# Retention in spans of 256 tokens, with the decay folded into the values and divided out by the head norm

## The chip, the cores and the metric

The kernel runs on one core of one Trainium2 chip, as one launch. The metric is device microseconds of that core, from the first to the last instruction of one execution; each kernel is run several times, and the median counts. One execution of each kernel is also recorded by the hardware profiler; all durations of single instructions are from that execution.

Five engines work side by side and wait for each other through semaphores: TensorE (PE, the matrix engine, with its weight load PEld), VectorE (DVE), ScalarE (ACT), GpSimd (POOL) and SyncE (SP, which here issues the DMA transfers). Matrix products are accumulated in PSUM banks of 128 x 512 float32.

## The reference

One encoder block on x [1, 1024 tokens, 1024], float32: a half-weighted SwiGLU, a token-mixing layer, a second half-weighted SwiGLU, a final norm. The change touches retention, in the token-mixing layer. It has 4 heads of 256 columns. Per head, with g = 1 - 2^(-5-h):

```
q = rotary(q); k = rotary(k) * 256**-0.5            # [1024, 256] each
inner_decay = g ** |n - m|     inside a chunk of 64 tokens
inner  = (q_chunk @ k_chunk.T * inner_decay) @ v_chunk
cross  = (q_i * g**(i+1)) @ state                   # state: 256 x 256
state  = state * g**64 + (k_i * g**(63-i)).T @ v_chunk
ret    = inner + cross
ret    = ret * rsqrt(mean(ret**2 over the head's 256) + 1e-6)
ret    = ret * silu(g_ret)
```

Written without the recurrence: token n of the output sums over every token m of its own chunk and of all chunks before, weighted by g^|n-m|. How many tokens are taken by the direct form (scores) and how many through the state is free, so long as whole chunks are kept together. After that `ret @ w_ret_up` and a pooling branch are merged by gates and go through an output projection.

## The kernel before, in words

Each matmul is done as three products of split operands (`mm3`, lines 159 to 163: high by high, high by low, low by high), so "one product" below is three matmul instructions. An operand is split by a CAST on ACT (line 141) and a subtraction on DVE (line 142), or, scaled on the way, by lines 145 (ACT) and 146 (DVE).

The stages in order are: SwiGLU 1, the projections (the last of them v), retention with the pooling branch beside it, the merge, the output projection (its first product is `ru0a`), SwiGLU 2. This text is about the retention stage. q, k, v and the swish gate g lie in DRAM and are loaded by head.

Retention goes by units: a head h and a half nh of the tokens (512), eight units in all, named by both digits ("20" is head 2, first half). For a unit the kernel before does:

- scores (line 1045): four key blocks of 128 tokens against the queries from that block on, 512, 384, 256 and 128 wide, two contractions of 128 each. Each goes to one bank `s`; DVE multiplies it by the decay (line 1053, `sc`), and it is split (`sm`).
- keys, first half only: `by_token` (line 996) transposes k into banks `kd..b` and splits it times a power of the decay; values: v likewise into banks `v..b` (transposes on PE against the identity `cst`).
- inner: ten blocks of scores by values, 256 wide, into two banks `ob`.
- across: in the first half the state `st` (keys by values, 8 products), in the second half the cross sum `xb` (queries by state, 8 products) in two banks of its own.
- outputs: in the first half ACT copies `ob` (line 1095); in the second ACT scales `xb` by the decay's power (line 1098) and DVE adds `ob` (line 1100). Then ACT sums squares (line 1103).
- after the second half, normalise: a reciprocal root by a few operations on [128 x 8] tiles, and eight scalings of the output on DVE (line 1110).
- finish, one unit later: the gate is loaded into a tile `rg`, the outputs are transposed in 16 transposes into four banks `ot` (line 1121), DVE multiplies bank by gate (line 1122), the result is stored to DRAM (`ret`) and loaded again by `take` for the output projection.

What sets the order: `Flow.run` (lines 51 to 81) takes steps of two parts, a preparation and a body, and runs each body four steps after its preparation, with some background work between. A scheduler then sets the order on each engine by its own picture of time, so two steps can be interleaved. Between the steps of retention stand fillers that need nothing of it: the pooling branch, 20 steps of 24 matmuls 512 wide each (4 of `px`, and 16 that make up `pu0` to `pu7`); their results are multiplied by a gate `pg` on DVE (line 975). In the kernel before one filler stands between the scores and the values of a unit, and one more behind `rest` in the first three units.

Memory that is handed round: six PSUM banks ("ps") for everything named above, two more ("sum") for running sums; in SBUF three tiles of tag `tl` (a unit's q, k and v, and the two gate tiles `rg` of a head), nine of tag `t4` (split scores, the state, the outputs, the reloaded `ret`), four of tag `raw` (weights before their split, gates `pg`), ten of tag `c2`. A tile's new owner waits until the old one's readers are done. All loads and stores named here are issued from SP, in order (line 129); a load whose tile is not free holds what is behind it.

Of the kernel before, what the change touches and what calls it, by code (L numbers as in the profile page):

```python
# [42 lines left out]
C_ID, C_ONE, C_CNT, C_KDEC, C_QDEC = 0, P, 2 * P, 2 * P + 64, 2 * P + 80  # L43
NC = 2 * P + 96
# [40 lines left out]
def block_kernel(ctx: ExitStack, tc, x, x_tok, vecs, f1_in, f1_out, w_in, pool_w, w_ret, w_pool, w_o,  # L85
# [98 lines left out]
    def inverse_root(sums, n, name):  # L184
# [7 lines left out]
        nc.vector.tensor_scalar(v, sums, 1.0 / n, EPS, MUL, ADD)  # L192
# [7 lines left out]
        tt(r, r1, t, MUL)  # L200
        return r
# [785 lines left out]
    def by_token(get, scale, name):  # L987

        slots = []
        for jj in range(2):  # L990
            b = bank(f"{name}b{jj}")
            m = mv(f"{name}{jj}")
            for z in range(2):
                for i in range(2):
                    j = 2 * jj + z
                    nc.tensor.transpose(b[:, z * HD + i * P : z * HD + (i + 1) * P], get(i)[:, j * P : (j + 1) * P],
                                        ident)
            for z in range(2):
                sl = slice(z * HD, (z + 1) * HD)
                split_scaled(m[:, 0, sl], m[:, 1, sl], b[:, sl], scale(2 * jj + z))  # L1000
            slots.append(m)
        return slots

    def col(t, n):
        return t[:, n : n + 1]

    class Unit:


        def __init__(self, h, nh):  # L1010
            self.h, self.nh, self.name = h, nh, f"{h}{nh}"

        def loads(self):
# [3 lines left out]
            for n, spilled in (("v", vs), ("q", qs), ("k", ks)):  # L1017
                r = self.src[n] = tl(f"{n}{self.name}")
                for i in range(2):
                    load(half(r, i), spilled[2 * self.h + i][:, at])  # L1020
            if self.nh == 0:
                self.dec = sb.tile([P, H], F32, tag="dec", bufs=1, name=f"dec{self.h}")
                load(self.dec, decay[self.h])
                self.ss = sb.tile([P, 8], F32, tag="ss", bufs=2, name=f"ss{self.h}")
                self.O = {}

        def follow(self, u):

            self.dec, self.ss, self.O, self.state = u.dec, u.ss, u.O, u.state

        def values(self):
            self.V = by_token(lambda i: half(self.src["v"], i), lambda j: col(mix.r_tok, 4 * self.nh + j),
                              f"v{self.name}")

        def keys(self):

            self.kd = by_token(lambda i: half(self.src["k"], i), lambda j: col(cst, C_KDEC + 4 * self.h + j),
                               f"kd{self.h}")
# [5 lines left out]
        def scores(self):  # L1044
            self.sm = []
            for j in range(4):
                wid = H - j * P
                b = bank(f"s{self.name}{j}")
                for i in range(2):
                    mm3(b[:, :wid], parts(self.K[i], slice(j * P, (j + 1) * P)), parts(self.Q[i], slice(j * P, H)),  # L1050
                        i == 0, i == 1)
                c = c2(f"sc{self.name}{j}")
                tt(c[:, :wid], b[:, :wid], self.dec[:, :wid], MUL)
                m = sb.tile([P, 2, H], F32R, tag="t4", bufs=N_T4, name=f"sm{self.name}{j}")
                split(m[:, 0, :wid], m[:, 1, :wid], c[:, :wid])
                self.sm.append(m)

        def cell(self, banks, t):
            return banks[t // 2][:, (t % 2) * HD : (t % 2 + 1) * HD]

        def v(self, j, at=None):
            o = (j % 2) * HD
            return parts(self.V[j // 2], slice(o, o + HD))

        def inner(self):
            self.ob = [bank(f"ob{self.name}{z}") for z in range(2)]
            for j in range(4):
                for t in range(j, 4):

                    mm3(self.cell(self.ob, t), parts(self.sm[j], slice((t - j) * P, (t - j + 1) * P)), self.v(j),  # L1070
                        j == 0 and t % 2 == 0, j == t)

        def across(self):
            if self.nh == 0:
                b = bank(f"st{self.h}")
                for i in range(2):
                    for j in range(4):
                        o = (j % 2) * HD + i * P
                        mm3(b[:, i * HD : (i + 1) * HD], parts(self.kd[j // 2], slice(o, o + P)), self.v(j),
                            i == 0 and j == 0, j == 3)  # L1080
                self.state = sb.tile([P, 2, H], F32R, tag="t4", bufs=N_T4, name=f"state{self.h}")
                split(self.state[:, 0], self.state[:, 1], b)
            else:
                self.xb = [bank(f"xb{self.h}{z}") for z in range(2)]
                for t in range(4):
                    for i in range(2):
                        mm3(self.cell(self.xb, t), parts(self.Q[i], slice(t * P, (t + 1) * P)),
# [279 lines left out]
```

## Time and profile before

| what | value |
| --- | --- |
| median of three runs | 2215.68 us (2214.87 to 2216.01) |
| span of the profiled execution | 2216.0 us |
| PE busy | 2192.6 us (99%), 10092 matmuls |
| DVE busy | 1637.3 us (74%) |
| ACT busy | 968.1 us (44%) |
| granted TensorE clock, mean of the span | 0.996 |
| retention stage: first transposes of v to the first `ru0a` | 1179.13 to 1402.80 us |

The profiled execution has no time of its own beside its span; the span of 2216.0 us stands 0.3 us above the median of the three runs.

How to read it: PE has hardly a gap over the whole span, so the time is the sum of what PE does, of the few times it waits, and of stretches at a lower clock. Matmuls are pipelined: one starts before the last has ended, so what a matmul costs is the distance from its start to the next one's start, and not its own duration. The view of windows gives busy time by engine for a stretch, with the granted clock (PEclk, 1.00 is full) and the DMA share; the view of waits says which engine waited for what, in total, how many times, and the longest; the timeline gives start, duration, engine, line, operation, and in brackets the idle time before and who ended it.

### The profile page before, as it was taken

The numbers are of one execution on the slowest core, as the hardware profiler recorded it, in microseconds if no ns is written. First come the engines' busy times: TensorE is split into PE (matmuls) and PEld (weight loads), VectorE is DVE, ScalarE is ACT, GpSimd is POOL, SyncE is SP. The second block draws the span as 40 slices with busy tenths as digits, with TensorE's granted clock in tenths as the row PEclk, the third lists the DMA queues.
The fourth block names the chain that finished last, engine by engine and source line by source line (L and its number), as shares of the span: only waits on it lengthen the run. The fifth ranks groups of instructions, "written<-read, shape, count | busy, mean of one in ns | idle before, by whom it ended". The sixth has DMA issues, their size and how long they took to land.

```text
span 2216.0 us, 27375 instructions
## 1 busy us (share of the span) xinstructions
PE 2192.6 (99%) x10092; PEld 1827.2 (82%) x10092; DVE 1637.3 (74%) x2706; ACT 968.1 (44%) x1722; POOL 0.2 (0%) x4
## 2 busy tenths in 40 slices
PE   9999999999999999999999999999999999999998
PEld 7888888888888888888888788888888888888887
DVE  8787777887696676777868567685876767788775
ACT  7533333455563434333437454443533333344451
POOL 0000000000000000000000000000000000000000
PEclk9999999999999999999999999999999999999999
DMA  5243232585323333232336457364132322249522
GB/s 209 95 162 138 91 124 91 181 309 190 114 96 128 124 114 124 96 129 80 133 114 215 127 181 262 105 218 134 57 143 100 123 92 103 95 159 330 181 89 77
DMA packets 109863, 311.87 MB, mean 141 GB/s; under 512 B 12320, under 2 KB 14496, under 8 KB 109728
## 3 DMA queue, kind: packets, MB, share of 16 engines
q1 hardware_dynamic: 109728, 310.12, 40.4%
q8 instruction: 79, 1.29, 0.2%
q14 instruction: 56, 0.46, 0.1%
HBM read 219.37 MB, written 90.70 MB: 140 GB/s over the span
## 4 chain that ended last, share of the span: by engine, by line
PE 97%; DVE 1%; DMA 1%; ACT 1%; issue 0%; SPq 0%; DVEq 0%; ACTq 0%
PE c_b L161 3%; PE c_b L162 3%; PE c_b L163 3%; PE a_b L161 3%; PE a_b L162 3%; PE a_b L163 3%; PE c_a L161 2%; PE a_a L162 2%; PE c_e L163 2%; PE c_a L163 2%; PE c_e L162 2%; PE a_e L162 2%; PE a_a L161 2%; PE a_e L161 2%; PE c_a L162 2%; PE a_a L163 2%
## 5 line engine op out<-in xcount | busy, mean ns | idle before, releaser
L141 ACT CAST c_wS<-c_S 128x512 fp32r<-128x512 f32 x88 | 54.7, 622 | 132.3 <-PE c_b L163 76.2
L141 ACT CAST a_wS<-a_S 128x512 fp32r<-128x512 f32 x84 | 52.3, 622 | 106.7 <-PE a_b L163 71.6
L142 DVE TENSOR_TENSOR c_wS<-c_S,c_wS 128x512 fp32r<-128x512 f32 x88 | 60.8, 691 | 25.1 <-ACT c_wS L141 24.5
L142 DVE TENSOR_TENSOR a_wS<-a_S,a_wS 128x512 fp32r<-128x512 f32 x84 | 58.0, 691 | 24.1 <-ACT a_wS L141 23.7
L161 PE MATMUL c_a<-n3R,c_wL 128*128 128x512 f32 x176 | 68.6, 390 | 0.0
L161 PE MATMUL c_b<-n3T,c_wS 128*128 128x512 f32 x176 | 68.5, 389 | 0.0
L163 PE MATMUL c_b<-n3T,c_wS 128*128 128x512 f32 x176 | 68.5, 389 | 0.0
L162 PE MATMUL c_b<-n3T,c_wS 128*128 128x512 f32 x176 | 68.5, 389 | 0.0
L162 PE MATMUL c_a<-n3R,c_wL 128*128 128x512 f32 x176 | 68.5, 389 | 0.0
L163 PE MATMUL c_a<-n3R,c_wL 128*128 128x512 f32 x176 | 68.5, 389 | 0.0
L161 PE MATMUL a_a<-n1R,a_wL 128*128 128x512 f32 x168 | 65.8, 391 | 0.0
L163 PE MATMUL a_a<-n1R,a_wL 128*128 128x512 f32 x168 | 65.4, 389 | 0.0
L162 PE MATMUL a_a<-n1R,a_wL 128*128 128x512 f32 x168 | 65.4, 389 | 0.0
L161 PE MATMUL a_b<-n1T,a_wS 128*128 128x512 f32 x168 | 65.4, 389 | 0.0
L162 PE MATMUL a_b<-n1T,a_wS 128*128 128x512 f32 x168 | 65.4, 389 | 0.0
L163 PE MATMUL a_b<-n1T,a_wS 128*128 128x512 f32 x168 | 65.4, 389 | 0.0
L141 ACT CAST c_wL<-c_ra 128x512 fp32r<-128x512 f32 x44 | 27.3, 621 | 44.2 <-PE c_e L163 38.0
L141 ACT CAST a_wL<-a_ra 128x512 fp32r<-128x512 f32 x42 | 26.0, 622 | 38.3 <-PE a_e L163 38.3
L142 DVE TENSOR_TENSOR c_wL<-c_ra,c_wL 128x512 fp32r<-128x512 f32 x44 | 30.4, 691 | 11.7 <-ACT c_wL L141 11.4
L162 PEld LDWEIGHTS c_b<-n3T,c_wS 128*128 128x128 f32 x176 | 33.0, 188 | 6.9
L161 PEld LDWEIGHTS c_b<-n3T,c_wS 128*128 128x128 f32 x176 | 33.0, 188 | 6.9
L162 PEld LDWEIGHTS c_a<-n3R,c_wL 128*128 128x128 f32 x176 | 33.0, 188 | 6.8
(2377 smaller groups left out, 7255.4 us busy)
## 6 DMA issues: line engine op xcount, KB each, us to landing
c_ra<-in_f_in SPq DMA_DIRECT2D x22, 512.0 KB, 3.6
c_rb<-in_f_in SPq DMA_DIRECT2D x22, 512.0 KB, 4.8
a_ra<-in_f_in SPq DMA_DIRECT2D x21, 512.0 KB, 3.7
a_rb<-in_f_in SPq DMA_DIRECT2D x21, 512.0 KB, 5.1
t<-au SPq DMA_DIRECT2D x11, 512.0 KB, 2.7
b<-an SPq DMA_DIRECT2D x11, 512.0 KB, 3.2
r<-au SPq DMA_DIRECT2D x11, 512.0 KB, 3.8
br<-r SPq DMA_DIRECT2D x11, 512.0 KB, 5.7
```

Source lines behind the costliest of these rows:

```text
L141: copy(hi, src)
L142: tt(lo, src, hi.bitcast(F32), SUB)
L161: mm(dst, w[0], m[0], start=start, stop=False, skip_group_check=True)
L162: mm(dst, w[0], m[1], start=False, stop=False, skip_group_check=True)
L163: mm(dst, w[1], m[0], start=False, stop=stop, skip_group_check=True)
```

## The change

The retention of a unit is cut into two spans of 256 tokens.

- Scores are only taken inside a span: two key blocks in each, so per unit one bank `sa` (256 wide twice) and one bank `sb` (128 wide twice), instead of four banks.
- All that comes before the span goes through the state. For every span but a head's first, queries by state are added into the same bank `ob` that holds the inner sum, so `xb`, its scaling (line 1098) and the addition (line 1100) are gone. For every span but a head's last, keys by values are added to the state's sum, which stays in one "sum" bank over a whole head; after each span it is split into operands (`state`).
- This needs no decay in between: v is scaled by g^-m (n counted from the middle of the head's 1024 tokens), plain k and q are used, the output comes out times g^-n, and the head norm divides it by its own root mean square. `inverse_root` gets two more [128 x 8] operations so that the epsilon is still right. The decay table of the scores now holds only what differs inside a span (the two-sided decay of a chunk, and zeros).
- Keys are transposed for three of four spans of a head (12 transposes, not 8).
- The order by steps is new: first span of unit n, scores of n+1, second span of n, transposes (values and keys) of n+1, then fillers (two behind each of the first two units, one behind the others), then `finish` of the head before. Four fillers stand ahead of the first unit.
- The gate tiles `rg` are taken from `t4`, not `tl`, but for the last head; the last head's result stays in SBUF and is not stored and loaded again.

The diff, cut to its core:

```diff
-        nc.vector.tensor_scalar(v, sums, 1.0 / n, EPS, MUL, ADD)
+        if by is None:
+            nc.vector.tensor_scalar(v, sums, 1.0 / n, EPS, MUL, ADD)
+        else:
+            tt(v, sums, by[0], MUL)
+            nc.vector.tensor_scalar(v, v, EPS, None, ADD)
...
+        if by is not None:
+            tt(r, r, by[1], MUL)
...
-            for n, spilled in (("v", vs), ("q", qs), ("k", ks)):
+            for n, spilled in (("q", qs), ("k", ks), ("v", vs)):
...
         def scores(self):
-            self.sm = []
-            for j in range(4):
-                wid = H - j * P
-                b = bank(f"s{self.name}{j}")
+            a, b = bank(f"sa{self.name}"), bank(f"sb{self.name}")
+            for dst, j, wid in ((a, 0, 2 * P), (b, 1, P)):
+                for z in range(2):
+                    o = (2 * z + j) * P
+                    for i in range(2):
+                        mm3(dst[:, z * wid : (z + 1) * wid], parts(self.K[i], slice(o, o + P)),
+                            parts(self.Q[i], slice(o, o + wid)), z == 0 and i == 0, i == 1)
...
+            tt(ca, a, self.dec, MUL)
...
+            split(self.sa[:, 0], self.sa[:, 1], ca)
+            split(self.sb[:, 0], self.sb[:, 1], cb[:, :HD])
...
+        def turned(self):
+            if self.nh == 0:
+                tt(self.vs, mix.r_tok, head(C_VDEC, self.h), MUL)
+            self.V, self.kt = [], []
+            for n, slots in (("v", self.V), ("k", self.kt)):
+                src = self.src[n]
+                for z in range(2):
+                    if n == "k" and self.nh == 1 and z == 1:
+                        continue
+                    b = bank(f"{n}t{self.name}{z}")
+                    m = mv(f"{n}t{self.name}{z}")
+                    for t in range(2):
+                        for i in range(2):
+                            o = (2 * z + t) * P
+                            nc.tensor.transpose(b[:, t * HD + i * P : t * HD + (i + 1) * P], half(src, i)[:, o : o + P],
+                                                ident)
+                    if n == "k":
+                        split(m[:, 0], m[:, 1], b)
+                    else:
+                        for t in range(2):
+                            sl = slice(t * HD, (t + 1) * HD)
+                            split_scaled(m[:, 0, sl], m[:, 1, sl], b[:, sl], col(self.vs, 4 * self.nh + 2 * z + t))
+                    slots.append(m)
...
+        def span(self, z, state, states):
+            ob = bank(f"ob{self.name}{z}")
+            for j, t, m, o in ((0, 0, self.sa, 2 * z * P), (0, 1, self.sa, 2 * z * P + P), (1, 1, self.sb, z * P)):
+                mm3(self.cell(ob, t), parts(m, slice(o, o + P)), parts(self.V[z], slice(j * HD, (j + 1) * HD)),
+                    j == 0 and t == 0, j == t and state is None)
+            if state is not None:
+                for t in range(2):
+                    o = (2 * z + t) * P
+                    for i in range(2):
+                        mm3(self.cell(ob, t), parts(self.Q[i], slice(o, o + P)),
+                            parts(state, slice(i * HD, (i + 1) * HD)), False, i == 1)
+            last = self.nh == 1 and z == 1
+            if not last:
+                begun = state is not None
                 for i in range(2):
-                    mm3(b[:, :wid], parts(self.K[i], slice(j * P, (j + 1) * P)), parts(self.Q[i], slice(j * P, H)),
-                        i == 0, i == 1)
...
-        def inner(self):
-            self.ob = [bank(f"ob{self.name}{z}") for z in range(2)]
-            for j in range(4):
-                for t in range(j, 4):
...
+                    for j in range(2):
+                        o = j * HD + i * P
+                        mm3(self.cell(states, i), parts(self.kt[z], slice(o, o + P)),
+                            parts(self.V[z], slice(j * HD, (j + 1) * HD)), not begun and i == 0 and j == 0, j == 1)
+                state = sb.tile([P, 2, H], F32R, tag="t4", bufs=N_T4, name=f"state{self.name}{z}")
+                split(state[:, 0], state[:, 1], states)
+            if z == 0:
+                self.O[self.nh] = t4(f"o{self.name}")
+            o = self.O[self.nh]
+            copy(half(o, z), ob)
+            for t in range(2):
+                junk = c2(f"junk{self.name}{z}{t}")
+                act(junk[:, :HD], o[:, z * H + t * HD : z * H + (t + 1) * HD], AF.Square,
+                    accum_out=col(self.ss, 4 * self.nh + 2 * z + t))
+            return state
...
+        def first(self, before):
             if self.nh == 0:
...
+                self.states, state = sum_bank(f"st{self.h}"), None
             else:
...
-        def outputs(self):
...
-            else:
-                for t in range(4):
-                    act(tiles[t], self.cell(self.xb, t), AF.Copy, scale=col(cst, C_QDEC + 4 * self.h + t))
-                for z in range(2):
-                    tt(half(o, z), self.ob[z], half(o, z), ADD)
...
+        def finish(self, last=False):
             for i in range(2):
                 await_stored(f"g{self.h}")
-                g = tl(f"rg{self.h}{i}")
+                g = (tl if last else t4)(f"rg{self.h}{i}")
                 load(g, gs[2 * self.h + i])
...
+                if last:
+                    up.tiles.update({(2 * self.h + i, j): half(g, j) for j in range(2)})
+                else:
+                    load(ret[2 * self.h + i], g)
...
-        yield units[0].operands, units[0].values
+        def first(n):
+            if n + 1 < len(units):
+                after = units[n + 1]
+                if after.nh == 1:
+                    after.follow(units[n])
+                after.operands()
+            units[n].first(units[n - 1])
+
+        def turned(n):
+            units[n].turned()
+            if n + 1 < len(units):
+                units[n + 1].loads()
+
+        yield units[0].operands, none
+        yield from fill()
+        yield none, units[0].scores
+        yield none, lambda: turned(0)
+        yield from fill(3)
         for n, u in enumerate(units):
...
-            def rest(u=u, after=after):
-                u.inner()
-                u.across()
-                if after:
-                    after.operands()
-                u.outputs()
...
-            yield none, scores
-            if u.nh == 0:
-                yield none, u.keys
-            yield from fill()
-            if after:
-                yield after.loads, after.values
-            yield none, rest
+            yield none, lambda n=n: first(n)
+            if n + 1 < len(units):
+                yield none, units[n + 1].scores
+            yield none, u.second
+            if n + 1 < len(units):
+                yield none, lambda n=n: turned(n + 1)
+            yield from fill(2 if n < 2 else 1)
             if u.nh == 0 and n:
                 yield none, units[n - 1].finish
-            if n < 3:
-                yield from fill()
...
+        yield none, take
         yield from fill(2)
-        yield none, units[-1].finish
-        yield none, lambda: take((6, 7))
+        yield none, lambda: units[-1].finish(True)
+        yield none, lambda: up.work(up.r22, up.t2, up.t1, up.t3, up.r21, up.p22, up.t4_)
...
+        consts[:, C_VDEC + at : C_VDEC + at + 8] = np.exp(-g * n) * HD**-0.5
+        consts[:, C_DSQ + at : C_DSQ + at + 8] = np.exp(2.0 * g * n) / HD
+        consts[:, C_DEC + at : C_DEC + at + 8] = np.exp(g * n)
```

How the order moves, at three places.

PE, between units 11 and 20. Before (`pu1d` is the end of a filler, `v20b` the transposed values of unit 20, and `ob` the first half of the inner sum of unit 11, scores `sm` by its values `v`):

```order
L459 MATMUL pu1d_10472<-po_10144,pu1w_10497 128x512
L996 MATMUL v20b_10500<-cst,v_10352 128x128 x4
L996 MATMUL v20b_10510<-cst,v_10352 128x128 x4
L161 MATMUL ob_10529<-v_10245,sm_10432 128x256
L162 MATMUL ob_10529<-v_10245,sm_10432 128x256
L163 MATMUL ob_10529<-v_10245,sm_10432 128x256
```

In the change (`state` by queries is the end of unit 11's second span; `vt` and `kt` are unit 20's transposes, `pu2d` a filler) the transposes:

```order
L163 MATMUL ob_10624<-state_10579,q_10314 128x256
L1065 MATMUL vt_10674<-cst,v_10467 128x128 x4
L1065 MATMUL vt_10684<-cst,v_10467 128x128 x4
L1065 MATMUL kt_10694<-cst,k_10464 128x128 x4
L1065 MATMUL kt_10702<-cst,k_10464 128x128 x4
L462 MATMUL pu2d_10474<-po_9765,pu2w_10530 128x512
L463 MATMUL pu2d_10474<-po_9765,pu2w_10530 128x512
```

and where that filler ends:

```order
L463 MATMUL pu2d_10475<-po_9828,pu2w_10530 128x512
L465 MATMUL pu2d_10474<-po_9825,pu2w_10530 128x512
L465 MATMUL pu2d_10475<-po_9828,pu2w_10530 128x512
L161 MATMUL ob_10766<-vt_10675,sma_10618 128x256
L162 MATMUL ob_10766<-vt_10675,sma_10618 128x256
L163 MATMUL ob_10766<-vt_10675,sma_10618 128x256
```

Before, the inner sum of unit 11, with all its operands made, stood right behind the transposes of the next unit. Now unit 11 is done when unit 20 is transposed, keys and values together, and a filler of 24 matmuls stands between these 16 transposes and the first inner sum of unit 20 (`vt` by `sma`).

SP, the loads of head 0's gate (from `g_196` and `g_197`; q, k and v of the numbers 176, 184, 192 and one above belong to head 2, `pg`, `pm` and `pu5raw` to fillers). Before:

```order
L129 DMA pg_11547<-gt_223 128x1024
L129 DMA pm_229<-pg_10726 128x1024
L129 DMA rg_10364<-g_196 128x1024
L129 DMA pu5raw<-in_w_pool 128x1024
L129 DMA rg_10379<-g_197 128x1024
L129 DMA ret_236<-rg_10364 128x1024
L129 DMA ret_237<-rg_10379 128x1024
```

And in the change:

```order
L129 DMA dec_10470<-in_decay 128x512
L129 DMA rg_10500<-g_196 128x1024
L129 DMA k_10464<-k_184 128x512
L129 DMA k_10464<-k_185 128x512
L129 DMA v_10467<-v_192 128x512
L129 DMA v_10467<-v_193 128x512
L129 DMA rg_10515<-g_197 128x1024
L129 DMA q_10710<-q_176 128x512
```

Before, both gate loads stood behind all loads of unit 20 and ahead of those of unit 21. Now the first stands ahead of unit 20's k and v, and the second behind them, ahead of unit 21's q.

DVE, around the operands of unit 21. Before, unit 21's operands (the scalings of head 1's outputs stand some rows further up, ahead of the first `v` rows):

```order
L146 SCALAR_TENSOR_TENSOR v_10737<-v21b_10736,n2r,v_10737 128x256
L146 SCALAR_TENSOR_TENSOR v_10747<-v21b_10746,n2r,v_10747 128x256
L142 TENSOR_TENSOR q_10828<-q_10523,q_10828 128x512
L142 TENSOR_TENSOR q_10831<-q_10523,q_10831 128x512
L142 TENSOR_TENSOR k_10834<-k_10526,k_10834 128x512
L142 TENSOR_TENSOR state_10825<-st_10800,state_10825 128x512
L142 TENSOR_TENSOR k_10837<-k_10526,k_10837 128x512
```

And in the change, the norm of head 1 (`ir1`, `o`), and unit 21's operands:

```order
L202 TENSOR_SCALAR ir1t<-ir1t 128x8
L142 TENSOR_TENSOR q_10753<-q_10710,q_10753 128x512
L204 TENSOR_TENSOR ir1r<-ir1r_10653,ir1t 128x8
L142 TENSOR_TENSOR q_10756<-q_10710,q_10756 128x512
L206 TENSOR_TENSOR ir1r<-ir1r,cst 128x8
L142 TENSOR_TENSOR k_10759<-k_10713,k_10759 128x512
L1123 TENSOR_SCALAR o_10349<-o_10349,ir1r 128x256 x4
L1123 TENSOR_SCALAR o_10582<-o_10582,ir1r 128x256 x4
L981 TENSOR_TENSOR pg_10743<-pu2d_10474,pg_10743 128x512
L981 TENSOR_TENSOR pg_10743<-pu2d_10475,pg_10743 128x512
L142 TENSOR_TENSOR k_10762<-k_10713,k_10762 128x512
L142 TENSOR_TENSOR state_10788<-st_10765,state_10788 128x512
```

The eight scalings of `o` and two gate products `pg` of a filler now stand between the first and the second operand of unit 21's keys.

More of the change, by code (lines that the diff above doesn't have):

```diff
@@ L984, in fillers, with head @@
         yield from pool_up()
[L987 to L992, printed above, removed]
-            for z in range(2):
[L994 to L1002, printed above, removed]
     def col(t, n):
         return t[:, n : n + 1]
+    def head(t, h):
+        return cst[:, t + 8 * h : t + 8 * h + 8]
     class Unit:
@@ L1024, in loads @@
                 self.ss = sb.tile([P, 8], F32, tag="ss", bufs=2, name=f"ss{self.h}")
+                self.vs = sb.tile([P, 8], F32, tag="vs", bufs=2, name=f"vs{self.h}")
                 self.O = {}
         def follow(self, u):
[L1029 to L1038, printed above, removed]
+            self.dec, self.ss, self.vs, self.O = u.dec, u.ss, u.vs, u.O
         def operands(self):
@@ L1073, in across @@
-        def across(self):
-            if self.nh == 0:
[L1075 to L1082, printed above, removed]
-            else:
-                self.xb = [bank(f"xb{self.h}{z}") for z in range(2)]
-                for t in range(4):
-                    for i in range(2):
-                        mm3(self.cell(self.xb, t), parts(self.Q[i], slice(t * P, (t + 1) * P)),
-                            parts(self.state, slice(i * HD, (i + 1) * HD)), i == 0 and t % 2 == 0, i == 1)
@@ new lines, in first, with second @@
+        def first(self, before):
+            if self.nh == 0:
+                self.states, state = sum_bank(f"st{self.h}"), None
+            else:
+                self.states, state = before.states, before.state
+            self.state = self.span(0, state, self.states)
+        def second(self):
+            self.state = self.span(1, self.state, self.states)
+            if self.nh == 1:
+                r = inverse_root(self.ss, HD, f"ir{self.h}", (head(C_DSQ, self.h), head(C_DEC, self.h)))
+                for nh in range(2):
+                    for t in range(4):
+                        sl = self.O[nh][:, t * HD : (t + 1) * HD]
+                        nc.vector.tensor_scalar(sl, sl, col(r, 4 * nh + t), None, MUL)
@@ L1129, in none, with take @@
         pass
-    def take(kts):
-        for kt in kts:
+    def take():
+        for kt in range(6):
             r = t4(f"ret{kt}")
```

68 lines of the change are left out of this document (18 added, 50 removed).

## The prediction

> **What bounds the kernel now.** The page comes first.
>
> ```profile
> span 2216.0 us, 27375 instructions
> PE 2192.6 (99%) x10092; PEld 1827.2 (82%) x10092; DVE 1637.3 (74%) x2706; ACT 968.1 (44%) x1722; POOL 0.2 (0%) x4
> PE 97%; DVE 1%; DMA 1%; ACT 1%; issue 0%; SPq 0%; DVEq 0%; ACTq 0%
> ```
>
> PE sets the time: it is busy 99% of the span, and the chain that ended last runs through PE for 97%. A change moves the time by what it takes off PE, by PE's waits, and by stretches at a lower clock. The profiled span stands 0.3 us above the median, so the sum is made against 2216.0. The diff touches the retention stage alone, whose windows come next (columns: length, busy time of PE, PEld, DVE, ACT, POOL, then PEclk, DMA share and GB/s).
>
> ```profile
> 1179.10:1402.80 223.70, 216.40 (x1266) 190.51 (x1264) 158.69 (x328) 122.39 (x285) 0.00 (x0) 0.98 0.55 181
> 1240.00:1290.00 50.00, 46.30 (x285) 40.63 (x283) 26.50 (x62) 21.08 (x56) 0.00 (x0) 0.97 0.53 174
> 1290.00:1330.00 40.00, 37.09 (x223) 33.03 (x223) 23.72 (x54) 18.32 (x51) 0.00 (x0) 0.91 0.50 162
> ```
>
> The stage lasts 223.7 us, with PE's clock down to 0.97 over 50 us and 0.91 over 40 us: 50 x 0.03 + 40 x 0.09 = 5.1 us lost, of which I take 4.6, since PE stood idle in a part of it. The waits of PE in the stage:
>
> ```profile
> PE ob L161 <- DVE v L146: 4.6, 2, 2.3
> PE pu0d L456 <- DVE sc L1053: 0.7, 1, 0.7
> PE v30b L996 <- DVE pg L975: 0.6, 1, 0.6
> PE v20b L996 <- DVE pg L975: 0.6, 1, 0.6
> PE s L161 <- DVE pg L975: 0.6, 1, 0.6
> PE st L161 <- ACT kd L145: 0.2, 1, 0.2
> ```
>
> Together 7.3 us. Two of 2.3 us carry most of it. The timeline shows what stands behind the first (the second, behind `v30b`, is the same a head later):
>
> ```profile
> 1243.37 0.60 PE L1121 MATMUL ot<-cst,o 128*128 128x128 f32 x4
> 1267.58 1.25 PE L996 MATMUL v20b<-cst,v 128*128 128x128 f32 x8 [0.56 <-DVE pg L975]
> 1268.86 0.32 SPq L129 DMA_DIRECT2D rg<-g  x1
> 1270.49 0.87 DVE L146 SCALAR_TENSOR_TENSOR v<-v20b,n2r,v 128x256 fp32r<-128x256 f32 x2
> 1271.12 0.36 PE L161 MATMUL ob<-v,sm 128*128 128x256 f32 x1 [2.28 <-DVE v L146]
> 1271.99 0.32 SPq L129 DMA_DIRECT2D rg<-g  x1
> 1273.08 1.29 DVE L1122 TENSOR_TENSOR rg<-ot,rg 128x512 f32<-128x512 f32 x2
> ```
>
> The outputs of head 0 are transposed into banks `ot` from 1243.37 on, but their gate is only loaded at 1268.86, when unit 20's transposes have released a `tl` tile, so the multiplication that frees these four of six banks starts at 1273.08. For 30 us scores, fillers, transposes and sums share two banks, and every owner waits for the one before: transposes for `pg` (0.56), unit 11's sum for the split of unit 20's values (2.28). The half clock follows right behind each of these two stalls.
>
> **The change part by part.** Matmuls are priced by the distance between starts:
>
> ```profile
> 1179.13 1.03 PE L996 MATMUL v00b<-cst,v 128*128 128x128 f32 x8
> 1179.92 0.48 PE L161 MATMUL s<-q,k 128*128 128x512 f32 x1
> 1181.38 0.33 PE L161 MATMUL s<-q,k 128*128 128x384 f32 x1
> 1182.44 0.28 PE L161 MATMUL s<-q,k 128*128 128x256 f32 x1
> 1183.15 0.22 PE L161 MATMUL s<-q,k 128*128 128x128 f32 x1
> 1183.77 0.41 PE L996 MATMUL kd0b<-cst,k 128*128 128x128 f32 x2
> 1401.66 0.39 PE L457 MATMUL pu7d<-po,pu7w 128*128 128x512 f32 x1
> 1402.80 0.39 PE L161 MATMUL ru0a<-ruR,ru0wL 128*128 128x512 f32 x1
> ```
>
> Eight transposes take 0.79 (0.099 each); six matmuls 384 wide 1.06 (0.177), 256 wide 0.71 (0.118), 128 wide 0.62 (0.103); five 512 wide take 1.14 (0.228). The groups give the counts before, over four heads:
>
> ```profile
> L161 PE MATMUL ob<-v,sm 128*128 128x256 f32 x80 | 25.0, 312 | 4.6 <-DVE v L146 4.6
> L161 PE MATMUL st<-v,kd 128*128 128x256 f32 x32 | 9.1, 285 | 0.2 <-ACT kd L145 0.2
> L161 PE MATMUL xb<-state,q 128*128 128x256 f32 x32 | 8.9, 279 | 0.0
> L161 PE MATMUL px<-pl,pw 128*128 128x512 f32 x32 | 12.6, 394 | 0.0
> L456 PE MATMUL pu5d<-po,pu5w 128*128 128x512 f32 x16 | 6.2, 389 | 0.0
> ```
>
> Each row has two like it (lines 162 and 163, or 457 and 459). Per head before: scores 12 matmuls of each width, 12 x (0.228 + 0.177 + 0.118 + 0.103) = 7.51; inner 60 x 0.118 = 7.08; state and cross 48 x 0.118 = 5.66; together 20.25, and 40 transposes (24 of k and v, 16 of the output) 3.96. After: scores 24 x 0.118 + 24 x 0.103 = 5.30; inner 36 x 0.118 = 4.25; state and cross 36 each, 72 x 0.118 = 8.50; together 18.05, and 44 transposes 4.36. The number of matmuls stays 156; they are narrower on the score side. Saved: 2.20 - 0.40 = 1.8 a head, **7.2 us**.
>
> The fillers (96 `px`, eight `pu` of 48: 480 x 0.228 = 109.4) stay. So the stage before is 4 x 24.2 + 109.4 = 206.2 of work, 7.3 of waits, 4.6 of half clock, and a rest of 5.6, the slower starts of some forty groups. I keep the rest, since there are about as many groups.
>
> The old waits go, with the half clock behind them. The gate now takes `t4` tiles: in SP's order its loads stand ahead of unit 20's k and v, nearly a unit ahead of the multiplication. A unit also needs fewer banks: two of scores, not four, and no `xb`. Removed DVE additions and ACT scalings lay beside PE and count nothing by themselves; the two new [128 x 8] operations a head stand ahead of the eight scalings, counted below.
>
> New waits come where a filler no longer covers the operands.
>
> ```profile
> L145 ACT ACTIVATE po<-px,vec 128x512 fp32r<-128x512 f32 x16 | 10.4, 698 | 0.9 <-PE px L163 0.9
> 1271.88 1.29 DVE L142 TENSOR_TENSOR k<-k,k 128x512 fp32r<-128x512 f32 x2
> 1285.05 2.19 DVE L1110 TENSOR_SCALAR o<-o,ir1r 128x256 f32<-128x256 f32 x8
> 1266.83 1.29 DVE L975 TENSOR_TENSOR pg<-pu1d,pg 128x512 f32<-128x512 f32 x2 [3.87 <-PE pu1d L459]
> 1197.55 0.28 PE L163 MATMUL st<-v,kd 128*128 128x256 f32 x1
> 1197.94 0.62 ACT L141 CAST state<-st 128x512 fp32r<-128x512 f32 x1
> 1198.83 0.68 DVE L142 TENSOR_TENSOR state<-st,state 128x512 fp32r<-128x512 f32 x1
> ```
>
> (a) Unit 01's operands are cast behind the last `po` of the pooling branch: about one `po`, 0.7 us. (b) Units 21 and 31: on DVE the second operand of k stands behind the eight scalings (2.19) and two `pg` (1.29). From the transposes to these scores DVE has 4 splits of v (1.74 by the row of 0.87 for two), 6 subtractions of k, q and transposed k (3.87), 2.19 and 1.29: 9.1, with about 1.6 for the norm's small operations and the start behind the first bank (an estimate), 10.7. PE has 16 transposes (1.6), 24 matmuls of filler (5.5), inner and state (21 x 0.118 = 2.5) and the first scores (0.35): 9.9. So 0.8 each, 1.6. Unit 11 has two fillers there, and no wait. (c) The state is now split after three spans of a head, 12 times in all, not 4. From its last matmul at 1197.55 to its operand at 1198.83 + 0.68 = 1199.51 pass 1.96 us. Inside a unit the scores of the next one (24 matmuls, 2.65) and the inner sum (9, 1.06) cover it with 3.7; between units transposes and a filler, 7. The last unit has no scores behind it: 1.96 less about 0.3 and less 1.06 leaves 0.6. Together 2.9 us; the bounds are nothing and the 11.9 (7.3 + 4.6) of before.
>
> Behind the last head, `rg` stays in SBUF: one store and load less, hidden behind four fillers of 5.5 us.
>
> **Sum**: 206.2 - 7.2 + 5.6 + 2.9 = 207.5, 16.2 less than 223.7: 2216.0 - 16.2 = 2199.8, on the median 2199.5; I say **2200 us**. With no new wait and half of the rest it is 2194; with twice these waits and one window of half clock 2206.
>
> **The rivals.**
>
> *The waits only move.* For it speaks DVE, busy 159 of 223.7 us, with the longest queue now just where a head ends; against it, the old waits hang on the banks `ot` held, which the new tiles release. If 11.9 us of waits and half clock come back elsewhere, only the matmuls are saved: 2216.0 - 7.2 = 2209 (2204 to 2213).
>
> *The clock drops behind the transposes.* The stall of 2.28 next to 8 transposes was followed by a half clock; the 0.6 to 0.7 us waits without one nearby were not. Now 16 transposes (1.6 us) stand together eight times; with a wait of 1.8 beside them PE is without a full matmul for 3.4 us, about what 1267.6 to 1271.1 was. At three heads' ends, a wait of 1.8 and 1.7 lost to the clock: 3 x 3.5 = 10.5, 2211. [...]
>
> *Slower: the state's hand-over is exposed.* Between the spans of a unit it needs 1.96 us on free queues and is covered by 3.7; if ACT's casts and DVE's subtractions of the next operands come first (four of each, 2.6 us, or 2.19 + 1.29 at a head's end), it comes 2 to 2.5 us late. At all eight units: 8 x 2.5 = 20, 2220. It decides from 2.0 us each (16.2 / 8). Against it, the state's subtraction stands ahead of the scores' in DVE's order at unit 11, and casts wait on loads issued a unit before.
>
> **How the numbers follow.** The forecast 0.56, better than 2194 0.03, waits that move 0.24, the clock 0.09, the hand-over 0.08. A change within 0.2% (4.4 us: above 2211.3) can't be told from none here. Faster: 0.56 + 0.03 + 0.19 of the 0.24 + 0.05 of the 0.09 = 0.83; same: 0.05 + 0.04 = 0.09; slower 0.08. The forecast's own range is 2194 to 2206; the range that holds 8 in 10 reaches to most of the moved waits and the clock, 2193 to 2212.
>
> **What would show it.** Right: `rg`'s multiplications follow their transposes within some 2 us and lose the wait for the gate; no PE wait over 1 us between units; PEclk 1.00 but for single windows; the stage near 207.5. Wrong: scores of units 21 and 31 waiting over 2 us for k's subtraction; cross sums waiting for `state`; PEclk at 0.9 near a head's end; waits of PE in the stage over 7 us in all.

## The result and the profile after

The changed kernel takes 2198.0 us, the median of four runs (2197.18 to 2200.49); the kernel before, beside it, 2215.85 us (2214.87 to 2216.16). The ratio is 0.992, with a 95% interval from 0.9906 to 0.9934: 17.9 us less. Five more runs on another occasion gave 2197.74.

The page of the changed kernel (the first two lines of it, and the chain that ended last):

```profile
span 2198.7 us, 27345 instructions
PE 2179.3 (99%) x10108; PEld 1818.6 (83%) x10108; DVE 1628.7 (74%) x2682; ACT 966.6 (44%) x1702; POOL 0.2 (0%) x4
PE 92%; DVE 3%; DMA 3%; ACT 1%; issue 1%; SPq 0%; DVEq 0%; ACTq 0%
```

PE still sets the time. The retention stage now runs from the first `px` (it stands ahead of the first scores) at 1180.15 to the first `ru0a` at 1385.53. Its window, with the columns as before:

```profile
1180.15:1385.53 205.38, 202.98 (x1282) 182.16 (x1280) 144.78 (x294) 115.24 (x256) 0.00 (x0) 1.00 0.52 180
```

205.4 us against 223.7, 18.3 less, and no stretch at a lower clock: PEclk is 1.00, where it was 0.98. All waits of PE in the stage:

```profile
PE px L161 <- DVE ca L1042: 1.7, 1, 1.7
PE sa L163 <- DVE k L142: 0.5, 2, 0.2
PE px L161 <- DVE kt L142: 0.2, 1, 0.2
```

2.4 us, where there were 7.3. The hand-over of a head's gate, on three engines (the answer to the seven rows on head 0 in the prediction):

```profile
1259.91 0.42 SPq L129 DMA_DIRECT2D rg<-g  x1
1264.43 0.42 SPq L129 DMA_DIRECT2D rg<-g  x1
1268.35 1.91 PE L1134 MATMUL ot<-cst,o 128*128 128x128 f32 x16
1268.99 2.48 DVE L1135 TENSOR_TENSOR rg<-ot,rg 128x512 f32<-128x512 f32 x4 [1.27 <-PE ot L1134]
```

The loads are issued 8.4 and 3.9 us ahead of the transposes, DVE waits for the transposes and not for the gate, and the four banks are free some 3 us after the transposes began, not after 30. Two waits of PE ahead of the stage (0.3 and 0.7 us in the first SwiGLU, at code that did not change) make the profiled execution about 1 us longer up to there; the sums below are made inside the stage. In every run that lists both, the time stands 1.7 to 2.2 us above the span, mostly 1.8. So the span of 2216.0 before stands for an execution of about 2217.8, some 2 us above the median, and was not, as the table of the profile before had it, 0.3 us above.

### The profile page after: what moved, and what is told of

The parts are those of the page before. It is cut to its first block, busy times and chain, and to the rows that moved or that the text cites. A ratio compares the mean times of both kernels' runs of the same rounds, so it can differ in the third digit from the quotient of the medians.

```text
span 2198.7 us, 27345 instructions
## 1 busy us (share of the span) xinstructions
PE 2179.3 (99%) x10108; PEld 1818.6 (83%) x10108; DVE 1628.7 (74%) x2682; ACT 966.6 (44%) x1702; POOL 0.2 (0%) x4
## 3 DMA queue, kind: packets, MB, share of 16 engines
q8 instruction: 79, 1.29, 0.2%
## 4 chain that ended last, share of the span: by engine, by line
PE 92%; DVE 3%; DMA 3%; ACT 1%; issue 1%; SPq 0%; DVEq 0%; ACTq 0%
PE c_b L161 3%; PE c_b L163 3%; PE c_b L162 3%; PE a_b L161 2%; PE a_b L162 2%; PE a_b L163 2%; PE c_a L161 2%; PE c_e L163 2%; PE c_a L163 2%; PE c_e L162 2%; PE c_e L161 2%; PE c_a L162 2%; PE a_e L162 2%; PE a_e L163 2%; PE a_e L161 2%; PE a_a L162 2%
## 5 line engine op out<-in xcount | busy, mean ns | idle before, releaser
L162 PEld LDWEIGHTS c_b<-n3T,c_wS 128*128 128x128 f32 x176 | 33.0, 188 | 6.9
L162 PEld LDWEIGHTS c_a<-n3R,c_wL 128*128 128x128 f32 x176 | 33.0, 188 | 6.9
L163 PEld LDWEIGHTS c_a<-n3R,c_wL 128*128 128x128 f32 x176 | 33.0, 188 | 6.9
```

What stands on the lines that cost most here:

```text
L162: mm(dst, w[0], m[1], start=False, stop=False, skip_group_check=True)
L163: mm(dst, w[1], m[0], start=False, stop=stop, skip_group_check=True)
```

## The experiments

All times are medians; the kernel before ran beside each group, at 2215.8 to 2216.2.

**Before, with only the gate's tile changed.**

```diff
-                g = tl(f"rg{self.h}{i}")
+                g = t4(f"rg{self.h}{i}")
```

> The kernel before, with only the gate tiles rg taken from t4 and not from tl (spans, products and the order of the steps stay as before). Theory (the late gate holds four of six banks, and the half clock follows the stall): the two waits of 2.3 us, the three of 0.6 us behind pg and the half clock of 4.6 us go, about 10 to 11 us, so about 2205 to 2206; PEclk is 1.00 through the stage. Rival (the banks are short anyway, with four score banks, two of ob and two of xb a unit, and only the cut into spans frees them): no more than 3 us go, 2213 or above, and PE still waits over 1 us at the transposes of units 20 and 30.

Measured: 2206.21 us (2206.11 to 2208.94), 0.9962 of before (0.9949 to 0.9974). The window of the stage, the waits of PE in it, and head 0's gate:

```profile
1178.59:1391.70 213.11, 209.30 (x1266) 186.57 (x1265) 158.21 (x328) 121.17 (x285) 0.00 (x0) 1.00 0.56 190
PE pu2d L456 <- DVE rg L1122: 1.7, 1, 1.7
PE pu3d L456 <- DVE rg L1122: 1.5, 1, 1.5
PE pu0d L456 <- DVE sc L1053: 0.7, 1, 0.7
...
1241.69 0.91 SPq L129 DMA_DIRECT2D rg<-g  x2
1242.58 0.60 PE L1121 MATMUL ot<-cst,o 128*128 128x128 f32 x4
1248.16 2.56 DVE L1122 TENSOR_TENSOR rg<-ot,rg 128x512 f32<-128x512 f32 x4 [4.06 <-DMA rg<-g]
```

One word of the code takes 10.6 us out of the stage (223.7 to 213.1) and 9.6 us off the median. The gate is now loaded when the transposes begin, and the banks are held for 8 us and not for 30. Both stalls of 2.3 us are gone, and the half clock with them. The theory holds. What it missed: the load still comes late by its own flight, and at the two next heads a filler now waits 1.5 to 1.7 us for an `rg` product to free a bank.

**The change, with the gate in `tl` again.**

```diff
-                g = (tl if last else t4)(f"rg{self.h}{i}")
+                g = tl(f"rg{self.h}{i}")
```

> The changed kernel, with the gate tiles of all heads taken from tl again. Theory (late gate): in SP's order the first gate of a head now comes behind the next unit's k and v and the second behind the store of the first, so ot banks stay held while the next unit goes on; stalls and half-clock windows come back at two or three heads' ends, 4 to 11 us: 2202 to 2209. Rival (a unit in spans needs so few banks that held ones don't matter): within 1.5 us of 2198.

Measured: 2204.83 us (2203.84 to 2208.06), 6.8 more than the change.

```profile
1179.19:1388.98 209.79, 204.42 (x1282) 182.35 (x1280) 143.77 (x291) 114.95 (x256) 0.00 (x0) 1.00 0.52 176
PE sa L163 <- DVE k L142: 2.7, 2, 1.5
PE vt L1065 <- DVE rg L1135: 0.9, 2, 0.5
...
1264.61 0.32 SPq L129 DMA_DIRECT2D rg<-g  x1
1274.03 0.32 SPq L129 DMA_DIRECT2D rg<-g  x1
1277.61 1.29 DVE L1135 TENSOR_TENSOR rg<-ot,rg 128x512 f32<-128x512 f32 x2 [1.29 <-DMA rg<-g]
1281.84 0.80 SPq L129 DMA_DIRECT2D k<-k  x2
1285.77 1.21 ACT L141 CAST k<-k 128x512 fp32r<-128x512 f32 x2 [1.24 <-DMA k<-k]
1286.42 0.69 DVE L142 TENSOR_TENSOR k<-k,k 128x512 fp32r<-128x512 f32 x1 [0.49 <-ACT k L141]
```

The second gate load is issued only at 1274.03, and its product comes at 1277.61, 11 us after the transposes (1266.51). The waits come to 5.3 us in all. There is no window of half clock in the profiled execution, which is the fastest of the five; three of the other four have a mean clock of 0.997 where it has 0.998, so for them a stretch of half clock is not excluded.

The forecast range was met, and the mechanism in part. The spans do with fewer banks: banks held longer cost tenths of a microsecond at each transpose. The larger cost, waits of 2.7 us at two units (0.5 in the change), comes by another path. The late gate holds the loads that stand behind it in SP's order. Unit 21's q is loaded at 1279.64 and its k at 1281.84 (1266.46 and 1280.26 in the change), ACT stands 1.24 us for k ahead of its cast (in the change it doesn't wait, and casts k at 1284.19), and DVE stands 0.49 us for that cast. The eight scalings, two `pg` and the second subtraction of k follow without a gap, and PE waits 1.23 us for it, not 0.23. At unit 31 the three waits are 1.48, 0.73 and 1.46 us. That DVE stood 1.29 us for the gate itself hardly counts there: its subtractions of q start at 1284.48, against 1284.30 in the change. This path is read from the trace and was not tried by itself.

**Scores moved behind the second span.**

```diff
-                yield none, units[n + 1].scores
+                pass
             yield none, u.second
             if n + 1 < len(units):
+                yield none, units[n + 1].scores
                 yield none, lambda n=n: turned(n + 1)
```

> The changed kernel, with the next unit's scores moved from between the two spans of a unit to behind the second, so that only the inner sum (1.06 us) covers the state's way through ACT and DVE inside a unit. By the price of the hand-over (1.96 us on free queues): 0.9 us exposed at each of eight units, about 7 us, 2205, with PE's waits on state rows. If the queues of ACT and DVE are not free there (the rival that was slower), 2 to 2.5 us each, 2214 to 2218. If the hand-over is shorter than it looks or the order is mended by the scheduler: within 2 us of 2198.

Measured: 2200.31 us (2199.70 to 2200.55), 2.3 more than the change, nearest to the third of the expectations. The two of its waits that the edit concerns:

```profile
PE kt L1065 <- DVE cb L1045: 1.6, 2, 0.8
PE ob L161 <- ACT state L141: 0.3, 1, 0.3
```

Waits for `state` stay at 0.3 us (some of under 0.1 us are not in the list), because the scheduler brings products of the scores forward into the gap: in this trace rows of `sa` stand between the first and the later products of queries by state. So the experiment did not lay the hand-over bare as its edit meant, and the price of 0.9 us each was not tested by it. What the list shows as the edit's cost is banks: transposes of keys wait 1.6 us for a score bank that DVE has yet to read.

**Two pooling steps ahead of the first scores.**

```diff
         yield units[0].operands, none
-        yield from fill()
+        yield from fill(2)
         yield none, units[0].scores
         yield none, lambda: turned(0)
-        yield from fill(3)
+        yield from fill(2)
```

> The changed kernel, with two pooling steps ahead of the first unit's scores and two behind its transposes (one and three in the change). The changed kernel's one long wait, 1.7 us of px for a bank that the first scores hold until DVE's multiplication (behind four subtractions of pl), should go: 2196 to 2197. If the wait only moves to the scores or to the first inner sum: within 0.7 us of 2198.

Measured: 2196.34 us (2195.41 to 2198.52).

```profile
PE px L161 <- DVE cb L1045: 1.0, 1, 1.0
```

In this profile, which is of the slowest of the five, the wait shrank from 1.7 to 1.0 and moved to the second score bank, `cb`; the two of 0.2 us for the second subtraction of k are as before. The gain of 1.4 to 1.7 us is as expected in size, and not wholly by the wait's end; a run spreads by 3 us here, so the split between the two stays open.

**The same, and the fillers dealt out by halves.**

```diff
-            yield from fill(2 if n < 2 else 1)
+            yield from fill(1 + n % 2)
```

> The changed kernel, with two pooling steps ahead of the first scores and two behind the first transposes, and the fillers behind the units dealt out as one after a head's first half and two after its second (two after units 00 and 01 and one after the others in the change). What is left of PE's waits in the stage (1.0 and 2 x 0.2 us with the pooling steps moved) should shrink to the 1.0: 0.4 to 0.8 us under the kernel with only the pooling steps moved, 2195.5 to 2196. If a head's first half needs its second filler (state, operands): 1 to 4 us above it.

Measured: 2195.41 us (2194.53 to 2196.82), 0.9 less than with the pooling steps moved alone, though the runs of the two overlap. With 20 steps of filler in both kernels, two now stand where a head ends, so where DVE has the norm to do. Once more, beside the change on one chip:

> The changed kernel as it is, once more, on the same chip as the others of this series, for the comparisons: 2198 us.

Measured: 2197.74 us (2197.54 to 2198.35).

> The kernel with two pooling steps ahead of the first scores and the fillers dealt out one and two by halves, beside the changed kernel on one chip: 2 to 2.6 us less than the changed kernel (its waits of 2.4 us in the stage are gone). If that was chance: within 0.7 us of it.

Measured: 2195.54 us (2195.18 to 2195.84), 2.2 us under the change, with no overlap of the runs. In the profiles of both of its runs the list of waits of PE in the stage is empty, where one of 1.0 us had been expected to stay. This version beats both kernels.

**Transposes made three times.**

```diff
-                            nc.tensor.transpose(b[:, t * HD + i * P : t * HD + (i + 1) * P], half(src, i)[:, o : o + P],
-                                                ident)
+                            for _ in range(3):
+                                nc.tensor.transpose(b[:, t * HD + i * P : t * HD + (i + 1) * P],
+                                                    half(src, i)[:, o : o + P], ident)
```

> The changed kernel, with each transpose of values and keys made three times into the same place (224 transposes more; 48 or 36 stand in a row, 4.75 or 3.6 us, where 16 or 12 stood). If transposes keep the clock up like other matmuls: 224 x 0.099 = 22.2 us more, 2220, and PEclk 1.00 in the stage. [...]

Measured: 2220.08 us (2219.36 to 2220.96, eleven runs), 22.1 above the change: 224 times 0.099. The timeline of PE at the end of unit 11, and a window over the stage up to 1407:

```profile
1288.13 2.78 PE L1066 MATMUL vt<-cst,v 128*128 128x128 f32 x24
1290.75 2.78 PE L1066 MATMUL kt<-cst,k 128*128 128x128 f32 x24
1293.29 0.47 PE L462 MATMUL pu2d<-po,pu2w 128*128 128x512 f32 x1
...
1180.00:1407.00 227.00, 226.92 (x1508) 206.93 (x1507) 147.80 (x294) 117.89 (x257) 0.00 (x0) 1.00 0.48 163
```

48 transposes stand in a row for 5.2 us (1288.13 to 1293.29), and the clock stays at 1.00 before, in and behind them. Of the stretch from 1290.28 to 1293.70, as long as one of the windows further below, transposes alone fill 3.0 us. In this run the added transposes cost what the prediction's 0.099 says (22.1 / 224), and rows of 48 of them did not lower the clock.

**A longer wait behind the transposes.**

```diff
             tt(ca, a, self.dec, MUL)
+            if self.name == "00":
+                for _ in range(2):
+                    tt(ca, a, self.dec, MUL)
```

> The changed kernel, with DVE's multiplication of unit 00's first score bank made three times (two more, about 0.65 us each), so that PE's wait for that bank, 1.2 to 1.7 us right behind 16 transposes (1.7 us), becomes about 2.5 to 3.0 us. If idle time of the length seen before (2.28 us) sets off the half clock: 1.3 us of wait and 1.7 of half clock, 2201, with a window of PEclk 0.50 after the wait. If transposes keep the clock up and this idle time is still short enough: 2199.3, PEclk 1.00.

Measured: 2199.14 us (2198.26 to 2201.41), 1.4 above the change beside it, PEclk 1.00 through the stage. The wait, and the two windows of 3.41 us on which it falls (on the windows' start, see below):

```profile
1191.50 0.47 PE L161 MATMUL px<-pl,pw 128*128 128x512 f32 x1 [2.29 <-DVE cb L1048]
...
1187.26:1190.67 3.41, 1.95 (x18) 1.71 (x17) 3.41 (x7) 3.29 (x7) 0.00 (x0) 1.00 0.41 142
1190.67:1194.08 3.41, 2.06 (x8) 1.45 (x9) 3.39 (x8) 2.69 (x7) 0.00 (x0) 1.00 0.89 312
```

A wait of 2.29 us, as long as that of before, right behind 16 transposes, and no half clock. With four more multiplications instead of two:

> As the run with two more multiplications, with four more: a wait of about 3.9 to 4.3 us. Theory (idle time of PE in a window of 3.4 us sets off the half clock, transposes count as work): a window of PEclk 0.50 of 3.4 us; 2.6 us of wait and 1.7 of half clock, 2202.3. If the half clock of the kernel before had another cause: 2200.6, PEclk 1.00.

Measured: 2199.63 us (2198.41 to 2200.24). The edit did not do what it was meant to: the scheduler moved `cb` ahead of most of the added multiplications, and products of the state ahead of a part of `px`, so the longest wait was 1.7 us, and PEclk is 1.00. The window with the most idle time of PE:

```profile
1187.16:1190.57 3.41, 1.69 (x15) 1.44 (x14) 3.41 (x7) 2.56 (x7) 0.00 (x0) 1.00 0.63 184
```

Now the windows of the kernel before, each ahead of a drop and the stretch of half clock behind it, and the nearest window of the change, with its wait of 1.7 us:

```profile
1267.97:1271.38 3.41, 1.13 (x9) 0.74 (x8) 3.22 (x8) 2.98 (x7) 0.00 (x0) 1.00 0.72 223
1271.38:1274.79 3.41, 3.41 (x18) 3.41 (x18) 2.99 (x5) 0.75 (x2) 0.00 (x0) 0.50 0.96 300
1308.93:1312.34 3.41, 1.66 (x10) 0.84 (x8) 3.00 (x6) 2.25 (x5) 0.00 (x0) 1.00 0.33 127
1312.34:1315.75 3.41, 2.32 (x11) 2.35 (x12) 3.41 (x7) 2.11 (x5) 0.00 (x0) 0.50 0.93 272
...
1188.86:1192.27 3.41, 1.70 (x15) 1.45 (x14) 3.41 (x7) 2.52 (x6) 0.00 (x0) 1.00 0.46 165
```

In the traces of the kernel before and of the change the stretches of full clock, and those of half clock that end inside the trace, are whole multiples of 3.413 us long: before, full from 11.86 to 1271.38 (369 of them), half to 1274.79 (1), full to 1312.34 (11), half to 1319.17 (2) and full to 2206.64 (260); in the change, full from 11.27 to 2188.97 (638). The windows here are counted in such steps from the moment the full clock is first granted. Before, PE was idle for 2.28 us (3.41 - 1.13) and 1.75 us (3.41 - 1.66) of a window, and the next one ran at half. Where it was idle 1.71 (the change), 1.72 (four more) or 1.46 and 1.35 in two neighbours (two more), the full clock stayed. So the length of a single wait does not decide: 2.28 us inside one window were followed by half clock, 2.29 us spread over two were not.

Nor does the idle time of a window decide alone. Both of these executions also drop to half clock ahead of their end, 9.4 us (before) and 9.7 us (the change), behind windows with 2.16 and 1.70 us of idle time. In the run with two pooling steps ahead of the first scores the window ahead of that drop has only 1.57 us of idle time (3.41 - 1.84), less than the 1.72 above:

```profile
2183.46:2186.87 3.41, 1.84 (x15) 1.58 (x13) 0.85 (x2) 0.42 (x1) 0.00 (x0) 1.00 0.00 0
2186.87:2190.29 3.42, 1.23 (x3) 0.50 (x2) 1.62 (x9) 0.20 (x1) 0.00 (x0) 0.50 0.00 0
```

In the trace of before every other window at full clock has 0.56 us of idle time or less; in that of the change the one with 1.71 has the most, and the drop came behind 1.70. Between 1.57 and 1.72 the busy time of the profile does not tell them apart, and what the clock goes by stays open. The ends of matmuls are modelled in that busy time: in the window ahead of the change's drop four matmuls only one column wide stand for 0.58 us of it.

**Twice the norm's scalings.**

```diff
                         nc.vector.tensor_scalar(sl, sl, col(r, 4 * nh + t), None, MUL)
+                for nh in range(2):
+                    for t in range(4):
+                        sl = self.O[nh][:, t * HD : (t + 1) * HD]
+                        nc.vector.tensor_scalar(sl, sl, 1.0, None, MUL)
```

> The changed kernel, with eight more scalings (by 1) on DVE behind the eight of each head's norm, 2.19 us a head. By the prediction's sum for units 21 and 31 (DVE's work up to the second operand of k is longer than PE's, and PE now waits 0.2 us at each): nearly all of 2.19 appears at two heads' ends, and none at the others, where two fillers or no scores follow: 4 us, 2202. If DVE has slack there (PE's waits there come from something else): within 1 us of 2198.

Measured: 2199.27 us (2197.71 to 2200.47), 1.3 to 1.5 above the change, with overlapping runs: between the two expectations. The profiled execution is the fastest of the five. In it the eight scalings by a constant take 1.71 us, and PE's wait at units 21 and 31 grows from 0.23 to 0.5 each:

```profile
PE sa L163 <- DVE k L142: 1.0, 2, 0.5
```

DVE's queue does end last there, as the prediction had it, but 0.27 of 1.71 us is exposed at each: the scheduler puts the first products of the second span's inner sum ahead of the scores that wait.

**The last head's result through DRAM.**

```diff
-                if last:
-                    up.tiles.update({(2 * self.h + i, j): half(g, j) for j in range(2)})
-                else:
-                    load(ret[2 * self.h + i], g)
+                load(ret[2 * self.h + i], g)
```

(with the two tiles loaded again ahead of the output projection's operands, as before the change)

> The changed kernel, with the last head's result stored to DRAM and loaded again ahead of the output projection, as before the change. By the prediction (hidden behind four fillers): within 1 us of 2198. Rival (the two stores and loads are on the path to the last operands of the first product): 3 to 8 us more, with PE waiting at the products that need the last head's tiles.

Measured: 2198.75 us (2197.93 to 2199.39), 0.8 to 1.0 above the change, at the edge of what runs tell apart. The waits in its stage are those of the change, 1.2 in place of 1.7. The store and load are hidden.

## Why the prediction was right, point by point

2200 was forecast, with its own range from 2194 to 2206, and 2198.0 came, by the mechanism that was named. The upper end of that range is not the sum of its terms: twice the new waits and one window of half clock, at the 1.7 us used in the rivals (half of the 3.41 us that the shorter stretch of half clock lasted before), give 2199.5 + 2.9 + 1.7 = 2204; the result lies well inside either. By its terms, in the stage (207.5 forecast, 205.4 measured):

- **The bound** (PE, by work, waits and half clock) was right: busy 99% before and after.
- **The matmuls, 7.2 us.** The counts are those of the code; the distances between starts in the change are what was read before. From the timeline of PE at the last unit:

```profile
1340.15 0.28 PE L161 MATMUL ob<-state,q 128*128 128x256 f32 x1
1341.53 0.28 PE L161 MATMUL st<-vt,kt 128*128 128x256 f32 x1
1342.95 0.28 PE L161 MATMUL ob<-vt,sma 128*128 128x256 f32 x1
1343.99 0.29 PE L161 MATMUL ob<-state,q 128*128 128x256 f32 x1
```

  Twelve cross products in 1.38 (0.115 each), twelve of the state in 1.42 (0.118), nine inner ones in 1.04 (0.116). No run took this term alone. From the kernel before with its gate in `t4` to the change, the stage loses 213.1 - 205.4 = 7.7 us, of which 1.5 are waits (3.9 to 2.4), which leaves 6.2 for the matmuls and the starts of groups together.
- **The old waits and the half clock, 11.9 us.** Right, and for the reason given: the gate's tile alone took 10.6 us out of the stage before. It was the larger part of the gain. One reading of the order was wrong: only the first of a head's two gate loads stands ahead of the next unit's k and v, the second stands behind them, and they come 8.4 and 3.9 us ahead of the transposes, not nearly a unit. That was still enough. The two parts overlap: the spans with the gate still in `tl` take 13.9 us out of the stage (223.7 to 209.8), so the `t4` tile is worth 10.6 without the spans and 4.4 with them in the profiled executions (9.6 and 6.8 by the medians).
- **The rest** (slower starts) was kept at 5.6; 205.4 - 199.0 - 2.4 leaves 4.0. This and the waits are the 2.1 us by which the stage was forecast too long.
- **New waits**, 2.9 forecast, 2.4 measured, but at other places: that the two sums are near is luck. (a) Unit 01's operands: 0.7 was expected and none came; the wait that came (1.7 us in the profiled execution, 1.1 in another of the same kernel) is `px` waiting for unit 00's score bank, because DVE does four subtractions of `pl` ahead of `ca`:

```profile
1188.72 2.49 DVE L142 TENSOR_TENSOR pl<-pl,pl 128x512 fp32r<-128x512 f32 x4
1191.12 0.68 DVE L1042 TENSOR_TENSOR ca<-sa,dec 128x512 f32<-128x512 f32 x1
```

  The step looked for operands that come late, and did not follow the banks of the first scores with one filler fewer ahead of them. (b) Units 21 and 31: 0.8 each was expected and 0.23 came. The timeline of PE and DVE there:

```profile
1279.19 1.03 PE L1065 MATMUL vt<-cst,v 128*128 128x128 f32 x8
1286.26 2.19 DVE L1123 TENSOR_SCALAR o<-o,ir1r 128x256 f32<-128x256 f32 x8
1288.36 1.28 DVE L981 TENSOR_TENSOR pg<-pu2d,pg 128x512 f32<-128x512 f32 x2
1289.56 0.69 DVE L142 TENSOR_TENSOR k<-k,k 128x512 fp32r<-128x512 f32 x1
1288.91 0.28 PE L161 MATMUL sa<-q,k 128*128 128x256 f32 x1
1290.30 0.38 PE L163 MATMUL sa<-q,k 128*128 128x256 f32 x1 [0.23 <-DVE k L142]
```

  DVE took about what was summed, 11.1 us from the first transposes (1279.19) to the end of that subtraction (1290.25), against 10.7. PE's side was too short: 0.35 us of scores were counted ahead of that operand, but products with the other operand, and with the high part of this one, need no subtraction, and nine of the 24 ran first, 1.2 us (1288.91 to 1290.30, less the wait). (c) The last unit: 0.6 was expected and none came, since two of a filler's matmuls were put into the gap.
- **The moved waits** (2209) did not come: the gate in `t4` frees the banks, as held against this rival, and the run with the gate back in `tl` shows how near it was, at 2204.8.
- **The clock behind transposes** (2211) is refuted by the run with three transposes for one: it cost their time (22.1 us) and nothing else, with PEclk at 1.00 through the stage. (16 of them stand together four times, at the heads' first halves, and not eight; at the second halves it is 12.)
- **The state's hand-over** (2220): no wait for `state` is in the list of the change. With the scores moved away it rose to 0.3 us. How large it would be on PE with nothing to put in between was not tried.
- **The store and load of the last head** are hidden, as said.

## What to carry to other kernels

Look at what else a late tile holds: a gate load that waited for an SBUF tile shared with other loads held four of six PSUM banks for 30 us, and one word in the code, taken by itself, was worth more than all the narrower matmuls. A late load also holds the loads behind it in its queue (with the gate in `tl`, unit 21's k was loaded at 1281.84, and at 1280.26 in the change), so look at those too. A short wait of PE was paid a second time through the clock here: 2.28 us of idle time inside one window of 3.41 us were followed by half clock for 3.41 us, 2.29 us over two windows by none. So look at how much idle time falls into one window, and not at each wait alone. When a wait for an operand is estimated behind a scheduler, count everything that PE can do without that operand (other operands, high parts, fillers), since that is what will be put there.

## What the runs showed of the hardware that was not expected

With each transpose made three times, rows of 48 transposes, 5.2 us long, left the clock at 1.00. Half clock came behind windows of 3.413 us with 1.57 us (two pooling steps ahead of the first scores), 1.70 (the change), 1.75, 2.16 and 2.28 us (before) of idle time; windows with 1.71 (the change) and 1.72 (four more multiplications) were not followed by it, nor was a wait of 2.29 us that fell onto two windows (two more). Eight scalings by a constant took 1.71 us on DVE, where eight by a column of scalars took 2.19 in the same run.
